# Low parts of split weights made by an accumulating DMA instead of a subtraction

## The chip, the cores and the metric

The kernel runs on one core of a Trainium2 chip. The metric is the device time of one execution in microseconds; the median of several runs is what counts, and a profile of one execution shows where the time goes. The engines are called PE (matrix product; PEld is its loading of weights), DVE (vector), ACT (scalar activation), POOL (GpSimd) and SP (issues DMAs).

## What is computed

Two transformer-like layers run over 128 context tokens and 512 latent tokens with the same weights. The layers differ in their mixer; both end in a gated feed-forward network (FFN) with a short convolution. All sizes are float32:

```python
for l in range(DEPTH):                      # DEPTH = 2, D_MODEL = 1024
    sh1, sc1, g1, sh2, sc2, g2 = split(silu(c) @ w_mod[l] + b_mod[l], 6)
    h = x * (1 + sc1) + sh1
    d = even_mixer(h) if l % 2 == 0 else odd_mixer(h)
    x = layernorm(ALPHA * x + g1 * d, ln1_g[l], ln1_b[l])
    h = x * (1 + sc2) + sh2
    z = dwconv(h @ w_up[l], conv_w[l], conv_b[l])      # 1024 -> 2 * 2816
    f = (silu(z[..., :D_FF]) * z[..., D_FF:]) @ w_down[l]
    x = layernorm(ALPHA * x + g2 * f, ln2_g[l], ln2_b[l])
```

The even mixer has an input projection, a spatial gate, pooling and an output projection; the odd mixer has a gated recurrence, attention with cached keys and an output projection.

## The kernel before

Every float32 product is made of three products of rounded numbers. An array x is split into a high part hi (x rounded to the type F32R) and a low part lo = x - hi. `mm3` (L150) then issues three matmuls for each pair of operands: hi times hi (L153), hi times lo (L154), lo times hi (L155). Activations are split where they are made. Weights come from HBM and are split as they are needed, each once, and this splitting is what the change touches.

A weight tile of 128 x 1024 (512 KB) passes through these steps. `want` (L112) puts its address on a queue; all weights of a stage are queued in the order of their use. `load` (L115) takes the next one and issues its DMA on SP into one of 4 buffers `r`. `prep` (L121) takes the oldest loaded tile and calls `split` (L96): ACT copies it with rounding into hi (L98), and POOL or DVE writes lo = r - hi (L101). Both parts lie in a pool of 12 buffers `w`, so six weights fit at a time. Which engine subtracts is chosen by the fourth argument of `want` or by the argument of `prep`; POOL is the default. `take` (L144) hands the oldest finished pair to the matmuls, and `pump` (L136) prepares ahead until `6 - hold[0]` pairs are ready. ACT, DVE and POOL each execute their instructions in order, so an instruction that waits holds up what stands behind it on its engine. A split runs under `high_priority`.

```python
    def prep(lo_eng=None):
        ...
        hi, lo = W(shape, F32R), W(shape, F32R)
        with tc.high_priority() if urgent[0] else ExitStack():
            i = split(hi, lo, raw, act, lo_eng or pool)
```

Only SP's order is written by hand (L44); the framework orders the instructions of the other engines by dependencies and priorities.

The stages follow each other: even mixer (0 to about 245 us in the profile), FFN of layer 0 (to about 750), odd mixer (to about 1110), FFN of layer 1 (to the end). In an FFN, PE alternates between up-projections, one weight and 48 matmuls at a time into two large PSUM buffers `A` (`ntile` L337; ACT and DVE make the convolution of one buffer in L527 to L529 and so free it), and down-projections of 3 or 4 weights held together (`down` L582, `project` L474). In a down-projection, or in an output projection (`out_proj` L613, two halves of four weights), every weight is used for all tokens, so buffers `w` become free only near its end. In the FFN of layer 0, DVE also works through the modulation of the next stages (L243). At the end of each stage stands a norm (`Norm`, L344): for each block of tokens DVE, POOL and ACT scale and shift it (L370 to L413), PE transposes it, and ACT and DVE split it (L430); the last block's rows are made by DVE in L392. A residual is scaled ahead on POOL in L449, and partial sums are added to it on POOL in L470.

Of the kernel before, what the change touches and what calls it, by code (L numbers as in the profile page):

```python
# [14 lines left out]
ALU = mybir.AluOpType  # L15
# [25 lines left out]
def tile_hybrid_trunk(ctx, tc, xT, x, vecs, tabs, wm0, wm1, wmT, crow, grow, lnrow, bs, w_u, w_v, w_p, w_s, w_pool, w_eo,  # L41
# [4 lines left out]
    dve, act, pe, pool, sp = nc.vector, nc.scalar, nc.tensor, nc.gpsimd, nc.sync  # L46
# [22 lines left out]
    def W(shape, dt=F32):  # L69
        return wpool.tile(shape, dt, tag="w", name=nm("w"))  # L70

    def R(shape):
        return rpool.tile(shape, F32, tag="r", name=nm("r"))
# [19 lines left out]
    def f(ap):  # L93
        return ap.bitcast(F32)

    def split(hi, lo, src, hi_eng, lo_eng):  # L96
        if hi_eng is act:
            act.copy(hi, src)  # L98
        else:
            hi_eng.tensor_copy(hi, src)  # L100
        return lo_eng.tensor_tensor(lo, src, f(hi), ALU.subtract)  # L101

# [1 line left out]
    queue = []  # L104
    ready = []
    loaded = []
    hold = [2]
    depth = [2]
    pin = [False]
    urgent = [True]  # L110

    def want(src, shape, scale=None, lo=None):  # L112
        queue.append((src, shape, scale, lo))

    def load():  # L115
        src, shape, scale, lo = queue.pop(0)
        raw = R(shape)
        sp.dma_start(raw, src)
        loaded.append((raw, shape, scale, lo))

    def prep(lo_eng=None):  # L121
        if not loaded:
            load()
        raw, shape, scale, lo_ = loaded.pop(0)
        lo_eng = lo_eng or lo_
        if scale is not None:
            dve.tensor_scalar(raw, raw, scale, ATTN_SCALE, ALU.mult, ALU.mult)
        hi, lo = W(shape, F32R), W(shape, F32R)
        with tc.high_priority() if urgent[0] else ExitStack():
            i = split(hi, lo, raw, act, lo_eng or pool)  # L130
        if pin[0]:
            tc.keep_in_program_order(i)
            pin[0] = False
        ready.append((hi, lo))
# [25 lines left out]
        pool.tensor_tensor(r, v, eps[:, 2:3], ALU.pow)  # L160
        return r

# [1 line left out]
    back = []  # L164

    def tick(n=1):
        for _ in range(n):
            while back:
                try:
                    next(back[0])  # L170
                    break
                except StopIteration:
                    back.pop(0)
# [2 lines left out]
        while len(back) > k:  # L176
            tick()

# [1 line left out]
    vec = cpool.tile([128, V_N], F32, name="vec")  # L180
    sp.dma_start(vec, vecs)
    ident = cpool.tile([128, 128], F32, name="ident")
# [9 lines left out]
    scr = [[dpool.tile([2, D], F32, name=f"scr{l}_{i}") for i in range(6)] for l in range(2)]  # L192
    SA1, SB1, SG1, SA2, SB2, SG2 = range(6)

# [1 line left out]
    def lnc(l, j):  # L196
        o = V_LN + (l * 4 + j) * 8
        return vec[:, o:o + 8].unsqueeze(1).to_broadcast([128, 2, 8])
# [5 lines left out]
    def rows_out(l, items):  # L204
        n = len(items)
        col = M([128, n, 2, 8])
        for q, (i, ap) in enumerate(items):
            dve.tensor_copy(col[:, q], ap)
        yield
        ps = B()  # L210
        pe.transpose(ps[:16 * n, :128], col.rearrange("p n s k -> p (n s k)"), ident)
        row = Tm([16 * n, 128])
        act.copy(row, ps[:16 * n, :128])
        for q, (i, ap) in enumerate(items):
            sp.dma_start(scr[l][i].rearrange("s (k f) -> (s k) f", f=128), row[16 * q:16 * q + 16, :])

    def finish_a(l):
        a, b, s = M([128, 2, 8]), M([128, 2, 8]), M([128, 2, 8])
        m = mc[l]
        dve.tensor_scalar(s, m[:, 1], 1.0, None, ALU.add)  # L220
        dve.tensor_tensor(a, s, lnc(l - 1, 2), ALU.mult)
        dve.tensor_tensor(b, s, lnc(l - 1, 3), ALU.mult)
        dve.tensor_tensor(b, b, m[:, 0], ALU.add)
        return rows_out(l, [(SA1, a), (SB1, b)])

    def finish_b(l):
        a, b, s = M([128, 2, 8]), M([128, 2, 8]), M([128, 2, 8])
        m = mc[l]
        dve.tensor_scalar(s, m[:, 4], 1.0, None, ALU.add)
        dve.tensor_tensor(a, s, lnc(l, 0), ALU.mult)  # L230
        dve.tensor_tensor(b, s, lnc(l, 1), ALU.mult)
        dve.tensor_tensor(b, b, m[:, 3], ALU.add)
        return rows_out(l, [(SA2, a), (SB2, b)])

    def mod_load(l, m, k, new):
        raw = new([128, D])
        sp.dma_start(raw, wmT[l, m * 8 + k])
        return raw

    def mod_cols(l, m, k, cb, raw):  # L240
        junk = Tm([128, D], mybir.dt.bfloat16)
        for s in range(2):
            op = dve.scalar_tensor_tensor(junk, raw, 1.0, cb[s], ALU.mult, ALU.mult, accum_out=mc[l][:, m, s, k:k + 1])  # L243
            if s == 0 and l == 1:
                tc.keep_in_program_order(op)

    def add_bm(l, m):
        dve.tensor_tensor(mc[l][:, m], mc[l][:, m], bmc(l, m), ALU.add)

    def mod_vec(l, ms, cb, new=R):  # L250
        todo = [(m, k) for m in ms for k in range(8)]
        raw = mod_load(l, *todo[0], new)
        yield
        for n, (m, k) in enumerate(todo):
            cur = raw
            if n + 1 < len(todo):
                raw = mod_load(l, *todo[n + 1], new)
            mod_cols(l, m, k, cb, cur)
            yield
            if k < 7:  # L260
                continue
            add_bm(l, m)
            if m == 1:
                yield from finish_a(l)
            elif m == 4:
                yield from finish_b(l)
            elif m == 2:
                yield from rows_out(l, [(SG1, mc[l][:, 2])])
            elif m == 5:
                yield from rows_out(l, [(SG2, mc[l][:, 5])])  # L270
            yield
# [44 lines left out]
    def ln_row(l, j):  # L316
        return bc_load(lnrow[:, (l * 4 + j) * D:(l * 4 + j + 1) * D])

# [1 line left out]
    def new_h():  # L320
        hi = [S([128, 2, T], F32R) for _ in range(4)]
        lo = [S([128, 2, T], F32R) for _ in range(4)]
        return hi, lo
# [14 lines left out]
        group(u, h, out, 0)  # L338
        group(u, h, out, 1)

# [1 line left out]
    ys = [None] * 5  # L342

    class Norm:  # L344
# [152 lines left out]
            norm.turn(4)  # L497
            pin[0] = True

# [1 line left out]
    def ffn(l, h):  # L501
        def plan():
            prev = None
# [124 lines left out]
                residual(norm)  # L628
        return nxt

# [1 line left out]
    def even_first(cb):  # L632
        want(w_v[0], [128, 2, 512])
        want(w_u[0], [128, D])
# [85 lines left out]
        for e in (dve, pool, dve):  # L720
            prep(e)
# [26 lines left out]
    def even_mixer(make_norm, nxt_sub):  # L748
# [28 lines left out]
        prep()  # L777
        load()
        prep(dve)
        back.append(mod_vec(0, (3,), cb, S))  # L780
        tick()
        for i in range(2, 5):
# [119 lines left out]
        nxt = out_proj(w_eo, ycat, gate, make_norm, nxt_sub, lambda i: pool_out(3, qs[3]) if i == 2 else None)  # L902
        return nxt, cb

# [1 line left out]
    def softplus_neg(lam):  # L906
        n = 8
        t, u, e, z, z2, s = (M([128, n]) for _ in range(6))
        dve.tensor_scalar(t, lam, -1.0, None, ALU.mult)
        dve.tensor_tensor(u, t, lam, ALU.max)  # L910
        act.activation(u, u, AF.Tanh, scale=1.0 / 32.0)
        dve.tensor_scalar(e, u, 1.0, None, ALU.add)
        dve.reciprocal(e, e)
        dve.tensor_scalar(u, u, -1.0, 1.0, ALU.mult, ALU.add)
        dve.tensor_tensor(e, e, u, ALU.mult)
        for _ in range(4):
            dve.tensor_tensor(e, e, e, ALU.mult)
        dve.tensor_scalar(z, e, 2.0, None, ALU.add)
        dve.reciprocal(z, z)
        dve.tensor_tensor(z, z, e, ALU.mult)  # L920
        dve.tensor_tensor(z2, z, z, ALU.mult)
        dve.tensor_scalar(s, z2, 1.0 / 17.0, 1.0 / 15.0, ALU.mult, ALU.add)
        for c in (13, 11, 9, 7, 5, 3, 1):
            dve.tensor_tensor(s, s, z2, ALU.mult)
            dve.tensor_scalar(s, s, 1.0 / c, None, ALU.add)
        dve.tensor_tensor(s, s, z, ALU.mult)
        dve.tensor_scalar(t, t, 0.0, None, ALU.max)
        dve.scalar_tensor_tensor(s, s, 2.0, t, ALU.mult, ALU.add)
        return s
# [10 lines left out]
    def odd_mixer(h):  # L940
# [98 lines left out]
        def rest(make_norm, nxt_sub):  # L1039
# [20 lines left out]
            raw = R([128, 2, 256])  # L1060
# [145 lines left out]
                qt.append(q)  # L1206
            uk = take()

            # attention: heads in pairs
            kts = [[[W([96, 896], F32R) for _ in range(2)] for _ in range(1 + hh)] for hh in range(2)]  # L1210
            for kt, e in zip(kts[0] + kts[1], ((dve, act), (dve, act), (dve, act))):
                for q in range(2):
# [96 lines left out]
            for n in range(len(steps) + 3):  # L1309
                if n < len(steps):  # L1310
                    j, hh, i = steps[n]
# [23 lines left out]
                if n >= 3:  # L1335
                    j, hh, i = steps[n - 3]
# [29 lines left out]
        eng.tensor_tensor(x1, a, b, ALU.subtract)  # L1366
        eng.tensor_tensor(x2, c, e, ALU.add)

# [1 line left out]
    def sub(maker, *args):  # L1370
        return lambda h: Sub(*maker(*args, h))

# [126 lines left out]
```

## Time and profile before

| | us |
|---|---|
| median of 3 runs | 1579.01 |
| the runs | 1576.65, 1579.01, 1590.5 |
| span of the profiled execution | 1581.2 |
| PE busy | 1473.5 |
| DVE busy | 1002.7 |
| POOL busy | 785.0 |
| ACT busy | 585.9 |

The span is that of one execution, from the first to the last instruction, and is the time against which sums are made here. Busy time is the union of an engine's instructions. A row of waits says for whom an engine sat idle. A row of a timeline gives start, duration, engine, line and operation, how many were merged (x), and in brackets how long the engine had been idle before it and what ended that.

### The profile page before, as it was taken

The numbers are of one execution on the slowest core, as the hardware profiler recorded it, in microseconds if no ns is written. First come the engines' busy times: TensorE is split into PE (matmuls) and PEld (weight loads), VectorE is DVE, ScalarE is ACT, GpSimd is POOL, SyncE is SP. The second block draws the span as 40 slices with busy tenths as digits, with TensorE's granted clock in tenths as the row PEclk, the third lists the DMA queues.
The fourth block names the chain that finished last, engine by engine and source line by source line (L and its number), as shares of the span: only waits on it lengthen the run. The fifth ranks groups of instructions, "written<-read, shape, count | busy, mean of one in ns | idle before, by whom it ended". The sixth has DMA issues, their size and how long they took to land. (4 is left out here: it accounts for less than half of the span.)

```text
span 1581.2 us, 21997 instructions
## 1 busy us (share of the span) xinstructions
PE 1473.5 (93%) x8741; PEld 1320.6 (84%) x8741; DVE 1002.7 (63%) x1432; ACT 585.9 (37%) x868; POOL 785.0 (50%) x564
## 2 busy tenths in 40 slices
PE   6889988899799999899979899998999999999997
PEld 3675868898799898887969788777999898999995
DVE  3485686577976778648688667858585342423347
ACT  3422354231323132324566465625334232322323
POOL 1132476634746466547367410576538816255444
PEclk9999999999999999999999899999999999999999
DMA  9345613243444353421220100352342421221311
GB/s 380 130 160 200 253 43 104 80 134 134 166 153 148 119 175 120 136 105 60 98 87 1 57 1 1 121 189 78 120 133 107 134 81 57 91 80 54 94 41 67
DMA packets 51734, 177.61 MB, mean 112 GB/s; under 512 B 6128, under 2 KB 6704, under 8 KB 51632
## 3 DMA queue, kind: packets, MB, share of 16 engines
q1 hardware_dynamic: 51632, 176.21, 32.6%
q8 instruction: 69, 1.13, 0.3%
q14 instruction: 33, 0.27, 0.1%
HBM read 170.71 MB, written 5.48 MB: 111 GB/s over the span
## 5 line engine op out<-in xcount | busy, mean ns | idle before, releaser
L101 POOL TENSOR_TENSOR w<-r,w 128x1024 fp32r<-128x1024 f32 (+2 forms) x148 | 369.8, 2508 | 465.6 <-ACT w L98 453.6
L153 PE MATMUL A<-s,w 128*128 128x258 f32 (+1 forms) x1672 | 525.9, 315 | 28.8 <-DVE t L529 19.2
L154 PE MATMUL A<-s,w 128*128 128x258 f32 (+1 forms) x1672 | 524.6, 314 | 3.8 <-DVE s L101 3.8
L155 PE MATMUL A<-s,w 128*128 128x258 f32 (+1 forms) x1672 | 523.9, 314 | 0.6 <-POOL w L101 0.6
L153 PEld LDWEIGHTS A<-s,w 128*128 128x128 f32 x1672 | 320.7, 192 | 41.0 <-issue 30.5
L98 ACT CAST w<-r 128x1024 fp32r<-128x1024 f32 (+3 forms) x184 | 186.6, 1029 | 389.1 <-PE B L154 168.3
L154 PEld LDWEIGHTS A<-s,w 128*128 128x128 f32 x1672 | 321.5, 192 | 7.7 <-DVE s L101 4.6
L155 PEld LDWEIGHTS A<-s,w 128*128 128x128 f32 x1672 | 320.8, 192 | 3.4 <-issue 2.5
L154 PE MATMUL B<-w,s 128*128 128x512 f32 (+2 forms) x734 | 283.2, 386 | 6.6 <-DVE w L101 6.6
L153 PE MATMUL B<-w,s 128*128 128x512 f32 (+2 forms) x734 | 283.5, 387 | 0.0
L155 PE MATMUL B<-w,s 128*128 128x512 f32 (+2 forms) x734 | 282.2, 384 | 0.0
L470 POOL TENSOR_TENSOR y<-y,t 128x512 f32<-128x512 f32 x120 | 183.0, 1537 | 112.9 <-DVE t L468 103.1
L528 DVE SCALAR_TENSOR_TENSOR t<-A,vec,t 128x641 f32<-128x641 f32 x88 | 77.7, 883 | 215.1 <-ACT t L527 210.2
L468 DVE TENSOR_TENSOR t<-B,s 128x512 f32<-128x512 f32 x160 | 108.7, 686 | 125.6 <-PE B L155 107.6
L243 DVE SCALAR_TENSOR_TENSOR t<-r,v 128x1024 bf16<-128x1024 f32 x112 | 185.2, 1658 | 2.9 <-DMA r<-in_wmT_dram 2.2
L154 PEld LDWEIGHTS B<-w,s 128*128 128x128 f32 x734 | 139.0, 189 | 34.4 <-DVE w L101 8.0
L155 PEld LDWEIGHTS B<-w,s 128*128 128x128 f32 x734 | 139.1, 190 | 27.4
L153 PEld LDWEIGHTS B<-w,s 128*128 128x128 f32 x734 | 139.1, 190 | 27.0 <-DVE t L468 0.2
L98 ACT CAST s<-t 128x642 fp32r<-128x642 f32 x60 | 43.8, 730 | 199.8 <-DVE t L538 166.9
L101 DVE TENSOR_TENSOR w<-r,w 128x1024 fp32r<-128x1024 f32 (+2 forms) x36 | 56.5, 1577 | 50.3 <-ACT w L98 50.2
L529 DVE SCALAR_TENSOR_TENSOR t<-A,vec,t 128x641 f32<-128x641 f32 x88 | 77.8, 885 | 2.7
L527 ACT ACTIVATE t<-A,vec 128x642 f32<-128x642 f32 x88 | 77.5, 881 | 5.0 <-PE A L155 4.5
(249 smaller groups left out, 1602.3 us busy)
## 6 DMA issues: line engine op xcount, KB each, us to landing
r<-in_w_up_dram SPq DMA_DIRECT2D x88, 512.0 KB, 3.6
r<-in_wmT_dram SPq DMA_DIRECT2D x56, 512.0 KB, 3.2
r<-in_w_dn_dram SPq DMA_DIRECT2D x44, 512.0 KB, 3.6
s<-scr SPq DMA_DIRECT2D x20, 512.0 KB, 6.6
s<-in_wm_dram SPq DMA_DIRECT2D x16, 512.0 KB, 9.3
r<-in_wm_dram SPq DMA_DIRECT2D x16, 512.0 KB, 4.4
s<-in_wmT_dram SPq DMA_DIRECT2D x8, 512.0 KB, 3.4
r<-in_w_eo_dram SPq DMA_DIRECT2D x8, 512.0 KB, 4.2
```

Of the source, the lines that this page charges most:

```text
L98: act.copy(hi, src)
L101: return lo_eng.tensor_tensor(lo, src, f(hi), ALU.subtract)
L153: pe.matmul(out, ah, bh, start=i == 0, stop=False)
L154: pe.matmul(out, ah, bl, start=False, stop=False)
L155: pe.matmul(out, al, bh, start=False, stop=i == n - 1)
L243: op = dve.scalar_tensor_tensor(junk, raw, 1.0, cb[s], ALU.mult, ALU.mult, accum_out=mc[l][:, m, s, k:k + 1])
L468: dve.tensor_tensor(t, ps, gate[stream(i)][:, sl], ALU.mult)
L470: pool.tensor_tensor(ys[i][:, sl], ys[i][:, sl], t, ALU.add)
L527: act.activation(t, z, AF.Identity, bias=cb, scale=w1)
L528: dve.scalar_tensor_tensor(t[:, 1:], z[:, :T - 1], w0, t[:, 1:], ALU.mult, ALU.add)
L529: dve.scalar_tensor_tensor(t[:, :T - 1], z[:, 1:], w2, t[:, :T - 1], ALU.mult, ALU.add)
```

## The change

From one point of the even mixer on (`through[0] = True`, after L779, when eight weights have been split), `prep` makes lo in another way, unless the weight is scaled first: ACT writes hi as before, ACT then writes lo = -hi, and a DMA issued by POOL adds the weight to lo, read from HBM a second time. The engine named in `want` no longer counts there; one named in `prep` still does. The remaining hunks of the diff delete comment lines.

```diff
+    through = [False]
@@ def load():
         sp.dma_start(raw, src)
-        loaded.append((raw, shape, scale, lo))
+        loaded.append((raw, shape, scale, lo, src))
@@ def prep(lo_eng=None):
-        raw, shape, scale, lo_ = loaded.pop(0)
-        lo_eng = lo_eng or lo_
+        raw, shape, scale, lo_, src = loaded.pop(0)
         if scale is not None:
             dve.tensor_scalar(raw, raw, scale, ATTN_SCALE, ALU.mult, ALU.mult)
         hi, lo = W(shape, F32R), W(shape, F32R)
         with tc.high_priority() if urgent[0] else ExitStack():
-            i = split(hi, lo, raw, act, lo_eng or pool)
+            if lo_eng or scale is not None or not through[0]:
+                i = split(hi, lo, raw, act, lo_eng or lo_ or pool)
+            else:
+                act.copy(hi, raw)
+                act.mul(lo, f(hi), -1.0)
+                i = pool.dma_start(lo, src, accum_op=ALU.add)
         if pin[0]:
             tc.keep_in_program_order(i)
             pin[0] = False
         ready.append((hi, lo))
@@ even_mixer
         prep(dve)
+        through[0] = True
         back.append(mod_vec(0, (3,), cb, S))
```

## Rows read from the trace of the kernel before

**Rows 1.** The page's first part: busy us (share of the span) xinstructions of each engine.

```profile
PE 1473.5 (93%) x8741; PEld 1320.6 (84%) x8741; DVE 1002.7 (63%) x1432; ACT 585.9 (37%) x868; POOL 785.0 (50%) x564
```

**Rows 2.** Who PE waited for: total us, times, longest us.

```profile
PE A L153 <- DVE t L529: 19.2, 9, 5.4
...
PE B L154 <- DVE w L101: 6.6, 4, 2.7
...
PE B L211 <- DVE m L208: 5.8, 5, 1.8
...
PE A L154 <- DVE s L101: 3.8, 1, 3.8
...
PE A L153 <- DVE t L826: 3.3, 1, 3.3
```

**Rows 3.** Windows: us, then PE, PEld, DVE, ACT, POOL busy, PEclk, DMA share, GB/s.

```profile
25.00:50.00 25.00, 20.95 (x140) 13.79 (x142) 10.42 (x23) 7.38 (x14) 4.70 (x2) 0.93 0.96 372
...
1175.00:1200.00 25.00, 25.00 (x171) 24.92 (x170) 18.19 (x21) 11.24 (x14) 9.79 (x4) 1.00 0.45 168
```

**Rows 4.** Groups by line and form: busy us, mean ns of one, idle before.

```profile
L101 POOL TENSOR_TENSOR w<-r,w 128x1024 fp32r<-128x1024 f32 x138 | 351.6, 2557 | 449.0 <-ACT w L98 437.1 <-DMA s<-in_wm_dram 11.8
...
L98 ACT CAST w<-r 128x1024 fp32r<-128x1024 f32 x170 | 175.6, 1047 | 382.0 <-PE B L154 168.3 <-PE A L154 124.8 <-DMA r<-in_w_up_dram 61.3
...
L101 DVE TENSOR_TENSOR w<-r,w 128x1024 fp32r<-128x1024 f32 x32 | 48.7, 1530 | 50.3 <-ACT w L98 50.2
...
L901 ACT ACTIVATE y<-y 128x1024 f32<-128x1024 f32 x5 | 5.2, 1056 | 1.9 <-DMA y<-in_x_dram 1.9
```

**Rows 5.** Timeline of POOL, DVE, ACT in the odd mixer's norm: start, us.

```profile
1105.21 10.28 POOL L101 TENSOR_TENSOR w<-r,w 128x1024 fp32r<-128x1024 f32 x4
...
1105.47 5.45 DVE L392 SCALAR_TENSOR_TENSOR t<-t,m,s 128x512 f32<-128x512 f32 x2
...
1104.55 1.05 ACT L98 CAST w<-r 128x1024 fp32r<-128x1024 f32 x1
```

**Rows 6.** Timeline of DVE in the last norm, where no weight is left.

```profile
1576.85 1.40 DVE L392 SCALAR_TENSOR_TENSOR t<-t,m,s 128x512 f32<-128x512 f32 x2
```

**Rows 7.** Timeline of DVE in the norms of the even mixer and of layer 0.

```profile
230.64 5.46 DVE L392 SCALAR_TENSOR_TENSOR t<-t,m,s 128x512 f32<-128x512 f32 x2
...
748.49 4.36 DVE L392 SCALAR_TENSOR_TENSOR t<-t,m,s 128x512 f32<-128x512 f32 x2
```

**Rows 8.** Timeline in the FFN of layer 0: DVE and the PE wait that follows.

```profile
404.60 2.56 DVE L243 SCALAR_TENSOR_TENSOR t<-r,v 128x1024 bf16<-128x1024 f32 x1
...
408.11 0.36 PE L153 MATMUL A<-s,w 128*128 128x258 f32 x1 [4.69 <-DVE t L529]
```

**Rows 9.** Timeline in the same stage: DVE beside POOL's scaling of the residual.

```profile
278.46 11.87 POOL L449 TENSOR_TENSOR y<-y,s 128x1024 f32<-128x1024 f32 x5
...
284.26 11.48 DVE L538 TENSOR_TENSOR t<-t,t 128x642 f32<-128x642 f32 x1
```

**Rows 10.** The core's span and mean granted clock.

```profile
core 0: 1581.2 us, clock 0.976
```

**Rows 11.** A window right behind that PE wait; columns as in rows 3.

```profile
408.60:412.00 3.40, 3.40 (x18) 3.40 (x18) 3.37 (x3) 2.33 (x3) 3.40 (x2) 0.51 0.10 39
```

**Rows 12.** Timeline of two places where weights come just in time.

```profile
1062.96 3.90 ACT L98 CAST w<-r 128x1024 fp32r<-128x1024 f32 x4 [21.04 <-PE B L154]
...
1064.05 2.81 DVE L101 TENSOR_TENSOR w<-r,w 128x1024 fp32r<-128x1024 f32 x2 [0.78 <-ACT w L98]
...
1542.43 1.60 DVE L101 TENSOR_TENSOR w<-r,w 128x1024 fp32r<-128x1024 f32 x1 [0.86 <-ACT w L98]
...
1066.70 0.39 PE L154 MATMUL B<-w,s 128*128 128x512 f32 x1
```

**Rows 13.** DMA issues: KB each, median us from issue to landing.

```profile
r<-in_w_up_dram SPq DMA_DIRECT2D x88, 512.0 KB, 3.6
...
s<-in_wm_dram SPq DMA_DIRECT2D x16, 512.0 KB, 9.3
```

## Prediction

> **What bounds the kernel now.** I read the page's busy times first. PE is busy for 1473.5 of 1581.2 us, so 107.7 us is all the idle time that any helper engine can give back; DVE, at 1002.7 us, is the busiest helper, POOL has 785.0 and ACT 585.9 [rows 1]. The cores' view adds that the mean granted clock is 0.976 [rows 10]. The clock has two levels, 1.2 and 2.4 GHz, so 2 x 0.024 x 1581.2 = 76 us ran at the lower one, and up to 38 us were lost by that. It falls behind idle stretches of PE: after the 4.69 us wait at 403 to 408 us [rows 8] the window shows 0.51 and 18 matmuls in 3.4 us [rows 11], where a full-speed window has 171 in 25 us, or 23 in 3.4 us [rows 3]. An idle microsecond of PE therefore often costs more than one.
>
> Then the waits of PE. The subtraction on POOL, the largest group outside PE with 138 x 2.557 us [rows 4], is hardly among them. What ends PE's idle time is DVE: 19.2 us for L529, 6.6 for low parts made on DVE, 5.8, 3.8 and 3.3 for smaller steps [rows 2]. The timelines show why DVE is late. In the odd mixer's norm L392 took 5.45 us for two instructions while POOL subtracted for 10.28 us [rows 5]; in the last norm, with no weights left, the same two took 1.40 us [rows 6]. In the FFN of layer 0, L243 took 2.56 us and L529, queued behind it, then released PE 4.69 us late [rows 8]. So a DVE instruction with two inputs in SBUF stands still while POOL reads SBUF. The Trainium skill's "SBUF — State Buffer" (Who interferes with whom) describes the shared port as an exclusive lock; the trace agrees, with 5.45 us against 1.40.
>
> **What the change removes.** From the code, 183 weights are queued, 8 are split before the switch and 3 are scaled, so 172 move: 140 from POOL and 32 from DVE. POOL loses about 140 x 2.56 = 358 us and DVE 32 x 1.53 = 49 us [rows 4], plus the time that it stands blocked. Five terms follow for PE.
>
> - Three norms: L392 falls to 1.40 us from 5.46, 4.36 [rows 7] and 5.45 [rows 5], together 15.27 - 4.20 = 11 us. PE waits at that point, so I take 11.
> - Behind the first of them PE waits 3.8 us for a low part on DVE [rows 2] that stands behind small blocked instructions: 4.
> - L529 in the FFN of layer 0: 19.2 us [rows 2], of which some 5 stem from L538 (11.48 us), blocked by POOL's L449 [rows 9], which stays. Of the other 14 I take 9, because POOL's L470 stays too.
> - The transposes of the modulation (5.8) and the gate's sum (3.3) [rows 2]: 6 of 9.
> - Clock: behind these gaps lie some 30 us at the lower level, as in [rows 11], at most 15 us lost. I take 10.
>
> Sum 40 us; if only half of the blocked time reaches PE it is 20, with all of it about 55 (11 + 4 + 14 + 9 + 15, rounded up).
>
> **What it adds on engines.** ACT writes 172 negated copies; the nearest row is a scaled 128 x 1024 ACT copy of 1.056 us (L901, [rows 4]), so 172 x 1.06 = 182 us at most, some tiles being smaller. In FFN stages this is covered: a weight is 48 matmuls, at 171 in 25 us 7.0 us [rows 3], in which ACT now works 11.24 / 25 x 7.0 = 3.1 us. Without that cover each copy would delay the convolution behind it by 1.06 us. In the norms ACT is on the path: three or four casts like the one at 1104.55 [rows 5] stand between ACT's critical steps, and half of the copies fall into its idle time. I take 2 us for each of three norms, 6 in all (0 to 12). POOL issues 172 DMAs. No DMA of POOL is in the trace; below lies nothing, above the subtraction that it replaces, 2.56 us, so POOL gains or stays even, and L470 behind an issue waits no longer than now, but for the 1.06 us that the copy makes POOL wait longer. I cost the issue's effect on the path at nothing, within a landing of 6 us below.
>
> **The late low parts.** This is the loss. The DMA reads 172 x 512 KB = 90 MB again; at 372 GB/s [rows 3] that is 1.4 us of all queues per tile, or twice that if lo is read as well. A plain load lands in 3.6 us, under full queues in 9.3 [rows 13]: these are the bounds for landing. I take 6: a load, plus 1.4 for the second read, plus 1 for the issue by POOL, being nearer to a load on half-empty queues. Low parts then come 1.06 + 6 = 7 us after the cast instead of 1.5 to 2.6. In FFN stages four pairs lie ready, 4 x 7.0 = 28 us ahead, and by the matching described below the shortest lead behind a down-projection is 11 us, so an extra 5 us is hidden there. It is not hidden where buffers `w` come free only at the end of a projection whose successor needs the next weight at once. At 1062.96 ACT casts, after 21 us of waiting for PE; the two DVE subtractions end at 1066.86; a matmul needing the first of them starts at 1066.70 [rows 12]. Matching every weight's subtraction to its first use, I count seven such places: the output projections of the even and the odd mixer (at 193, 1039 and 1067 us), the last down-projection of each layer (711 and 1545, the latter [rows 12]), one recurrence gate (807) and the attention's value weight (884). At each PE would be late by 7.06 - 1.6 = 5.5 us, and lose 1.7 us more while the clock is down (3.4 us at half, [rows 11]): 7 x 7.2 = 50 us. PE need not stand still, though: other token blocks and the weights at hand fill it for about 4 us, and the framework orders PE itself. I take half, 25 us; bounds are 10 (landing 3.6, mostly covered) and 72 (landing 9.3, nothing covered: 7 x (1.06 + 9.3 - 1.6 + 1.7) = 73).
>
> The Trainium skill prices this landing otherwise: "DMA: Bandwidth & Descriptors" (Anatomy of one DMA) has 2.0 us plus bytes over 436 GB/s for a DMA from GpSimd, an estimate of 3.2 us for 512 KB, and "Collectives: The Full Stack" (The bandwidth ceiling) halves the rate for an add, an estimate of 4.4 us. By 4.4 us the seven places cost 7 x 5.6 = 39, half of it 19, and the time would come to about 1564, inside the forecast's own range. No row here shows such a DMA.
>
> **The sum.** -40 + 6 + 25 = -9 us, against the span of 1581.2: 1572. The median of the runs lies 2.2 us below that execution (1579.0), so I say 1570. One per cent, 15.8 us, is about what a measurement of this kernel can tell from no change; the forecast is that the two cancel nearly.
>
> **Rivals.**
>
> 1. The late parts are hidden. PE's order, remade for the slower arrival, covers the seven places, and the loss falls to 10: -40 + 6 + 10 = -24, or with the full 55 us of gain -39, so 1540 to 1555. For it: DVE's blocking is plain in rows 5 to 9, and the seven places have work of other blocks at hand. Against it: PE B L154 waits 6.6 us for `w` even now [rows 2].
> 2. Landing decides against it. At the seven places four raw loads start as soon as the casts free their buffers, and the low parts share the queues with them. With no cover, the loss reaches 50 (no better than even with the gain of 40 - 6 = 34, slower by 1% from 34 + 16 = 50 on) at a landing of 6 us; with half of it covered, from about 13. At 9.3 us without cover: -40 + 6 + 73 = +39, 1618; with a third covered, about 1594 to 1600. For it: 9.3 us is measured in the opening, whose queues are 0.96 busy [rows 3, 13]. Against it: the rest runs at half that share or less.
> 3. The issue on POOL blocks DVE as the subtraction did, so the gain fails and the losses stay: 6 + 25 = +31, 1610. No row shows a POOL DMA; against it, it moves no tile through POOL.
> 4. The transfers bind. If one held all queues for longer than the 7.0 us of a weight, less 1.4 for its load, the FFN stages would slow with each weight: at 8 us, 132 weights x 2.4 = 317 us. I give that 3 in 100.
>
> **Chances and range.** Forecast (nearly cancelled, 1556 to 1590): 0.42. Rival 1: 0.30. Rival 2: 0.20. Rival 3: 0.05. Rival 4: 0.03. The likeliest case's own range is 1556 to 1590; the range for 8 in 10 takes in rival 1 and the near part of rival 2: 1538 to 1605. Faster by over 1% is a time below 1563: rival 1 and a small part of the forecast, 0.35. Slower by over 1% is above 1595: 0.26. Within: 0.39.
>
> **What the profile after would show.** POOL's L101 on `w` gone but for the first and the scaled weights, L392 at 1.4 us in all norms, L243 at about 1.2 us, PE's wait for L529 down to some 10 us. ACT near 765 us busy. New waits of PE at L154 and L155 for a DMA of `w`, at the seven places, 2 to 6 us each. If these waits are absent, rival 1 holds; if they exceed 6 us, rival 2; if L392 still takes over 4 us, rival 3; if PE in the FFN of layer 1 drops from its 25.00 us in 25 [rows 3], rival 4. The forecast is wrong above all if a landing takes less than 4 or more than 10 us, or if the remade order of the engines moves the norms by itself.

## The result

The changed kernel takes 1638.95 us (median; 1636.06 to 1644.11) against 1584.12 us for the kernel before on the same chip (four runs, among them the three whose median was 1579.01). The ratio is 1.037, with a 95% interval of 1.032 to 1.042: slower by 3.7%, where 1570 was forecast. Times of the experiments below are also compared by the ratio to the kernel before on their own chip; one point (0.01) is 15.8 us. Runs in the chip's slower state are left out of times and ratios; only e14 had one.

The page's first part of the kernel after, its mean clock, and its DMA queues (packets, MB, share of 16 engines' span), to be read beside [rows 1, 10]:

```profile
PE 1488.2 (91%) x8741; PEld 1334.6 (82%) x8741; DVE 879.4 (54%) x1400; ACT 751.5 (46%) x1040; POOL 571.9 (35%) x596
```

```profile
core 0: 1634.3 us, clock 0.956
```

```profile
q1 hardware_dynamic: 51632, 176.21, 30.8%
q0 software_dynamic: 24768, 88.75, 30.7%
```

Every helper did what the change asked: DVE lost 123 us of work, POOL 213, ACT gained 166. Yet PE's idle time rose from 107.7 to 1634.3 - 1488.2 = 146.1 us, and PE is busy 14.7 us longer for the same 8741 matmuls, while 2 x 0.044 x 1634 = 144 us of the span now run at the lower clock (76 before). These two, 38.4 + 14.7, are the whole 53.1 us between the spans. In the queues' rows, the new queue of POOL holds the 16 engines as long as all plain loads together, with half their bytes: 0.307 x 16 x 1634.3 / 24768 = 0.324 us for a packet.

Who PE waited for (total us, times, longest us), beside [rows 2]:

```profile
PE A L158 <- DVE t L534: 22.1, 6, 7.1
PE B L432 <- POOL t L418: 16.2, 5, 5.1
PE B L159 <- DMA w<-in_w_dn_dram: 15.0, 4, 10.7
PE B L159 <- DMA w<-in_w_oo_dram: 11.7, 3, 4.9
...
PE B L159 <- DMA w<-in_w_uv_dram: 6.8, 1, 6.8
PE A L160 <- DMA w<-in_w_rg_dram: 5.7, 1, 5.7
PE B L159 <- DMA w<-in_w_eo_dram: 5.3, 4, 3.1
...
PE B L159 <- DMA w<-in_w_qkv_dram: 4.3, 3, 2.5
```

All instructions of the new line L135 together: who waited for its DMAs (us, times), and the time from issue to landing:

```profile
PE B L159: 43.1, 15
...
PE A L160: 8.6, 2
...
DMA to landing us min/median/max: 4.0/7.5/15.6
```

Two costs stand out, then. PE waits 51.7 us, at 17 places, for a low part itself. And L534 still holds PE for 22.1 us (L529 held it for 19.2 before), though DVE no longer stands still beside subtractions of POOL, as its steps in the norms show; beside [rows 5, 7]:

```profile
240.10 0.78 DVE L397 SCALAR_TENSOR_TENSOR t<-t,m,s 128x512 f32<-128x512 f32 x1 [1.78 <-POOL m L165]
241.13 0.73 DVE L397 SCALAR_TENSOR_TENSOR t<-t,m,s 128x512 f32<-128x512 f32 x1
...
758.77 1.40 DVE L397 SCALAR_TENSOR_TENSOR t<-t,m,s 128x512 f32<-128x512 f32 x2
```

The other old cause is still there, and it makes the longest of the six waits. While POOL scales the residual (L454), DVE's L543 stands still as L538 did in [rows 9], L534 comes late behind it, and PE waits (timelines of DVE and PE):

```profile
271.51 10.37 DVE L543 TENSOR_TENSOR t<-t,t 128x642 f32<-128x642 f32 x1
...
289.26 0.55 PE L158 MATMUL A<-s,w 128*128 128x258 f32 x1 [7.15 <-DVE t L534]
```

What else holds L534 now is seen in a timeline of the FFN of layer 0 (start, us, engine, line; the engines one after the other), and behind it the time to landing of the one load in it:

```profile
427.61 1.04 ACT L133 CAST w<-r 128x1024 fp32r<-128x1024 f32 x1 [5.73 <-DMA r<-in_w_dn_dram]
428.56 0.88 ACT L532 ACTIVATE t<-A,vec 128x642 f32<-128x642 f32 x1
...
429.47 0.89 DVE L533 SCALAR_TENSOR_TENSOR t<-A,vec,t 128x641 f32<-128x641 f32 x1 [6.74 <-ACT t L532]
430.39 0.89 DVE L534 SCALAR_TENSOR_TENSOR t<-A,vec,t 128x641 f32<-128x641 f32 x1
...
414.43 0.33 SPq L119 DMA_DIRECT2D r<-in_w_dn_dram  x1
...
431.43 0.55 PE L158 MATMUL A<-s,w 128*128 128x258 f32 x1 [6.40 <-DVE t L534]
```

```profile
DMA to landing us min/median/max: 13.1/13.1/13.1
```

Read it backwards. PE starts at 431.43 after 6.40 us, because DVE's convolution (L533, L534) came late. DVE waited 6.74 us for ACT's L532. L532 itself waited for nothing: it stood in ACT's queue behind a cast of the next weight, and that cast waited 5.73 us for a plain load that had been issued at 414.43 and took 13.1 us to land. Four of the six waits, 14.3 us, have this form. So the new DMAs delay PE through the loads of other weights. The landing times of the large transfers (KB each, median us) say the same. Before, the raw loads of w_up took 3.6 us [rows 13], and those of w_dn:

```profile
r<-in_w_dn_dram SPq DMA_DIRECT2D x44, 512.0 KB, 3.6
```

After, with the new DMAs between them:

```profile
r<-in_w_up_dram SPq DMA_DIRECT2D x88, 512.0 KB, 5.4
w<-in_w_up_dram POOLq DMA_DIRECT2D x88, 512.0 KB, 7.9
...
r<-in_w_dn_dram SPq DMA_DIRECT2D x44, 512.0 KB, 7.8
```

The other new waits are plainer. In a norm (timeline of ACT, POOL and PE):

```profile
234.21 1.04 ACT L134 ACTIVATE w<-w 128x1024 fp32r<-128x1024 f32 x1
...
235.55 0.91 POOL L135 DMA_DIRECT2D w<-in_w_up_dram  x1 [4.69 <-ACT w L134]
236.18 1.57 POOL L415 TENSOR_TENSOR t<-y,s 128x512 f32<-128x512 f32 x1
237.83 1.73 POOL L418 TENSOR_TENSOR t<-t,s 128x512 f32<-128x512 f32 x1
...
239.61 1.12 PE L432 MATMUL B<-ident,t 128*128 128x128 f32 x4 [5.13 <-POOL t L418]
```

POOL stood 4.69 us at the issue of a DMA that needs ACT's negated copy, and the norm's own L415 and L418 stood behind it. And in the FFN of layer 1 the longest wait of all:

```profile
1253.88 7.45 POOL L454 TENSOR_TENSOR y<-y,s 128x1024 f32<-128x1024 f32 x3
1261.27 0.87 POOL L135 DMA_DIRECT2D w<-in_w_dn_dram  x1
...
1270.41 0.80 PE L159 MATMUL B<-w,s 128*128 128x512 f32 x1 [10.65 <-DMA w<-in_w_dn_dram]
```

The negated copy was done at 1259.52 (ACT's L134 began at 1258.48 and took 1.04). POOL, busy with scaling the residual, issued the DMA at 1261.27, and it landed about 9 us later.

### The profile page after: what moved, and what is told of

It reads as the page before. It is cut to its first block, busy times and chain, and to the rows that moved or that the text cites. A ratio compares the mean times of both kernels' runs of the same rounds, so it can differ in the third digit from the quotient of the medians.

```text
span 1634.3 us, 22380 instructions
## 1 busy us (share of the span) xinstructions
PE 1488.2 (91%) x8741; PEld 1334.6 (82%) x8741; DVE 879.4 (54%) x1400; ACT 751.5 (46%) x1040; POOL 571.9 (35%) x596
## 3 DMA queue, kind: packets, MB, share of 16 engines
q0 software_dynamic: 24768, 88.75, 30.7%
## 4 chain that ended last, share of the span: by engine, by line
PE 62%; DMA 12%; DVE 10%; POOL 7%; ACT 5%; issue 4%; SPq 0%; DVEq 0%; POOLq 0%; ACTq 0%
PE A L158 12%; PE A L160 12%; PE A L159 12%; PE B L159 7%; PE B L160 7%; PE B L158 7%; POOL y L454 2%; DVE t L248 2%; DMA r<-in_w_dn_dram 1%; DMA w<-in_w_dn_dram 1%; DMA r<-in_wm_dram 1%; DMA w<-in_w_eo_dram 1%; PE B L1280 1%; DMA r<-in_w_up_dram 1%; DMA t<-in_lnrow_dram 1%
## 5 line engine op out<-in xcount | busy, mean ns | idle before, releaser
L158 PE MATMUL A<-s,w 128*128 128x258 f32 (+1 forms) x1672 | 527.2, 316 | 26.4 <-DVE t L534 22.1
L133 ACT CAST w<-r 128x1024 fp32r<-128x1024 f32 (+2 forms) x172 | 177.4, 1032 | 383.8 <-PE B L159 179.6
L159 PE MATMUL B<-w,s 128*128 128x512 f32 (+2 forms) x734 | 290.0, 395 | 36.3 <-DMA w<-in_w_dn_dram 15.0
L158 PE MATMUL B<-w,s 128*128 128x512 f32 (+2 forms) x734 | 285.8, 392 | 5.5 <-ACT s L1108 3.8
L160 PE MATMUL B<-w,s 128*128 128x512 f32 (+2 forms) x734 | 286.4, 391 | 0.0
L533 DVE SCALAR_TENSOR_TENSOR t<-A,vec,t 128x641 f32<-128x641 f32 x88 | 77.9, 885 | 300.4 <-ACT t L532 300.4
L159 PEld LDWEIGHTS B<-w,s 128*128 128x128 f32 x734 | 142.2, 194 | 70.1 <-DMA w<-in_w_dn_dram 16.8
L134 ACT ACTIVATE w<-w 128x1024 fp32r<-128x1024 f32 (+2 forms) x172 | 178.7, 1039 | 1.7
L135 POOL DMA_DIRECT2D w<-in_w_up_dram x88 | 77.3, 908 | 288.5 <-ACT w L134 282.9
L158 PEld LDWEIGHTS B<-w,s 128*128 128x128 f32 x734 | 141.4, 193 | 34.6 <-ACT s L1108 4.1
L160 PEld LDWEIGHTS B<-w,s 128*128 128x128 f32 x734 | 142.4, 194 | 27.5
L248 DVE SCALAR_TENSOR_TENSOR t<-r,v 128x1024 bf16<-128x1024 f32 x112 | 154.8, 1386 | 0.7
L135 POOL DMA_DIRECT2D w<-in_w_dn_dram x44 | 38.0, 864 | 232.1 <-ACT w L134 221.6
L534 DVE SCALAR_TENSOR_TENSOR t<-A,vec,t 128x641 f32<-128x641 f32 x88 | 77.9, 885 | 2.7
```

Of the source, the lines that this page charges most:

```text
L133: act.copy(hi, raw)
L134: act.mul(lo, f(hi), -1.0)
L135: i = pool.dma_start(lo, src, accum_op=ALU.add)
L158: pe.matmul(out, ah, bh, start=i == 0, stop=False)
L159: pe.matmul(out, ah, bl, start=False, stop=False)
L160: pe.matmul(out, al, bh, start=False, stop=i == n - 1)
```

## The experiments

Three theories stood at the start: low parts come too late (1), ACT's second copy holds up norms and convolutions (2), and the traffic slows the raw loads (3). Two more came up on the way: the accumulation costs queue time (4), and each accumulating DMA has a fixed price (5). In each diff the lines replace those of the changed kernel, if nothing else is said.

**What the relief is worth, and what a DMA takes back.**

```diff
 e1_copy_only
-                act.mul(lo, f(hi), -1.0)
-                i = pool.dma_start(lo, src, accum_op=ALU.add)
+                i = act.mul(lo, f(hi), 2.0 ** -12)
 e2_early_plain_read
-                act.mul(lo, f(hi), -1.0)
-                i = pool.dma_start(lo, src, accum_op=ALU.add)
+                i = pool.dma_start(lo, src)
 e5_plain_read_waits
-                i = pool.dma_start(lo, src, accum_op=ALU.add)
+                i = pool.dma_start(lo, src)
```

> The changed kernel without its second read: ACT still writes a second tile per weight (a small multiple of the high part), but no DMA adds to it, so the low part is left out. Theory 1, the low parts come too late (PE's waits for a DMA of w sum to 51.6 us after the change): with them gone only the relief of DVE and POOL and the ACT copies stay, so about 1550 us (1584 - 40 + 6), and no PE wait for w over 2 us. Theory 2, ACT's second copy holds up the norms and the convolutions: the waits for L418 (16.2 us) and L534 (22.1 us) stay, and the time is 1575 to 1590.

> The second read stays, 512 KB per weight from POOL's queue, but as a plain read that waits for no cast and no ACT copy; the low part is then the whole weight, so the subtraction is left out. Theory 1 (late low parts): the read is early, so the loss goes and the time is 1545 to 1565. Theory 3, the traffic itself costs (raw loads w_up 3.6 to 5.4 us and w_dn 3.6 to 7.8 us to landing): ACT's casts and the convolutions behind them stay late, L534 stays near 22 us, and the time is 1595 or more.

> The changed kernel with a plain read in place of the accumulating one: the cast, the negated copy and the wait for it stay, but the DMA overwrites the low part with the whole weight, so the subtraction is left out. It splits the 75 us between the early plain read (1564) and the change (1639). Theory 1, the wait for the cast and the copy makes the parts late: 1615 to 1639. Theory 4, it is the accumulation (30.7% of the queues' time against 18.0% for the plain read of the same bytes): 1580 to 1600.

Measured: e1 1537.0 us, ratio 0.970 (0.966 to 0.975); e2 1563.6 us, 0.987 (0.986 to 0.989); e5 1575.9 us, 0.995 (0.992 to 0.997). The relief of DVE and POOL is real, 47 us with ACT's copies already paid, more than the 34 forecast; PE still waited up to 3.4 us for a part that ACT had just written, where theory 1 allowed 2. The early plain read was as theory 1 had it. The surprise is e5: a plain DMA of the same bytes, that waits for the same copy, still beats the kernel before. Theory 1 expected 1615 or more. So the wait for the copy does not by itself make the loss; 4.2 points, 67 us, lie between a plain and an accumulating DMA at the same place (63 by the medians). Some of this is lateness all the same, because the accumulating DMA lands later: 51.7 us of PE's waits for a low part are 32.3 in e5.

```profile
PE B L159: 27.4, 9
...
PE A L160: 4.9, 1
```

The layer-0 stage shows the difference best, cut from the first transposition of its norm to that of the next (windows: us, then PE, PEld, DVE, ACT, POOL busy, clock, DMA share, GB/s); in this order before, after, e1, e5:

```profile
208.00:726.00 518.00, 483.04 (x2817) 447.90 (x2815) 371.98 (x501) 157.84 (x201) 300.98 (x158) 0.98 0.37 123
```

```profile
215.00:736.00 521.00, 487.50 (x2817) 453.93 (x2815) 328.84 (x500) 222.48 (x268) 186.57 (x161) 0.96 0.73 189
```

```profile
196.00:676.00 480.00, 472.42 (x2813) 441.16 (x2812) 318.21 (x499) 222.84 (x267) 133.87 (x93) 1.00 0.40 133
```

```profile
203.00:689.00 486.00, 474.90 (x2821) 442.51 (x2820) 320.44 (x500) 222.75 (x267) 167.90 (x161) 0.99 0.61 202
```

This stage gives 38 us to e1 and loses 36 of them again between e5 and the change: the DMA engines go from 0.61 to 0.73 busy for the same bytes (486 us at 202 GB/s and 521 at 189 are both 98 MB). In e1 and e5 the wait for the convolution is almost gone:

```profile
PE A L157 <- DVE t L533: 0.8, 1, 0.8
```

```profile
PE A L158 <- DVE t L534: 4.3, 3, 3.2
```

All stages in us, cut in the same way, the last one up to PE's last matmul:

| | even mixer | layer 0 | odd mixer | layer 1 |
|---|---|---|---|---|
| before | 207.7 | 518.2 | 356.0 | 488.8 |
| after | 214.6 | 521.2 | 383.1 | 504.8 |
| e1, no DMA | 195.5 | 480.6 | 351.2 | 491.7 |
| e2, early plain read | 207.3 | 491.5 | 357.4 | 497.1 |
| e5, plain read | 203.4 | 485.4 | 373.4 | 497.9 |
| e13, read and write | 210.8 | 517.3 | 382.6 | 505.7 |
| e12, below | 194.6 | 501.1 | 356.2 | 488.8 |

In the odd mixer and in layer 1 it is otherwise: 17 of the 27 us and 9 of the 16 are lost with the plain read already. In the odd mixer that is the part of theory 1, for the same read without the wait takes 357.4 us (e2) or, with a copy that only the matmuls wait for (e6), 361.3. In layer 1 it is not: these take 497.1 and 496.1.

**ACT's second copy.**

```diff
 e3_copy_and_subtract
-                i = pool.dma_start(lo, src, accum_op=ALU.add)
+                i = (lo_ or pool).tensor_tensor(lo, raw, f(lo), ALU.add)
 e6_early_read_and_copy
-                act.mul(lo, f(hi), -1.0)
-                i = pool.dma_start(lo, src, accum_op=ALU.add)
+                act.mul(hi, f(hi), 1.0)
+                i = pool.dma_start(lo, src)
```

> The kernel before plus the ACT copy: the high part is negated by ACT as in the change, and POOL or DVE then adds the raw tile onto it, in place of the DMA. No second read. Theory 1 (late low parts): the copy delays a low part by about 1.05 us and is mostly hidden, 1584 to 1596. Theory 2 (ACT's copy in front of the norms and convolutions): 1600 to 1620.

> The early plain read with a second ACT pass over each weight that nothing but the matmuls waits for (the high part is rewritten in place); the low part is the whole weight, so the subtraction is left out. Theory 1 (lateness of the read decides): 1564 to 1575. Theory 2 (ACT's second pass delays norms and convolutions, once raw loads are slower too): 1590 or more.

Measured: e3 1601.7 us, 1.011 (1.008 to 1.014); e6 1568.6 us, 0.991 (0.989 to 0.994). Where POOL's work must wait for the second copy it costs 17.6 us in all, and PE's wait for L418 grows from 9.1 to 22.8 us (that for low parts from 8.5 to 12.1); where only the matmuls wait for it (e6 against e2), some 6. Most of the copy's price is therefore the waiting of POOL's queue, not ACT's time. Theory 2 is right in e3 and too dear in e6.

**Which weights, and how early.**

```diff
 e4_tight_on_dve
-            if lo_eng or scale is not None or not through[0]:
+            if lo_eng or lo_ or scale is not None or not through[0]:
 e7_negate_first
-                act.copy(hi, raw)
-                act.mul(lo, f(hi), -1.0)
-                i = pool.dma_start(lo, src, accum_op=ALU.add)
+                act.mul(lo, raw, -1.0)
+                i = pool.dma_start(lo, src, accum_op=ALU.add)
+                act.copy(hi, raw)
 e11_load_one_ahead
-    depth = [2]
+    depth = [3]
 e14_negate_from_raw
-                act.mul(lo, f(hi), -1.0)
+                act.mul(lo, raw, -1.0)
```

> The changed kernel, but the 32 weights whose low part DVE subtracted before are subtracted by DVE again; 140 keep the DMA. Theory 1 (late low parts): these are the weights used soon after their buffers come free (w_dn, w_eo, w_oo, w_qkv), so PE's waits for a DMA of w fall from 51.6 to about 20 us and the time to about 1600. Theory 3 (traffic): a fifth less traffic, 1625 or more.

> The change with ACT's two passes exchanged: minus the high part is made first, straight from the raw tile, then the high part. Every accumulating DMA can start one ACT pass (1.05 us) earlier. Theory 1 (lateness): seven or so places with 1.05 us less wait and a shorter spell at the lower clock, 1622 to 1632. Theory 3 or 4 (traffic or accumulation): 1635 to 1643.

> The changed kernel with three raw tiles loaded ahead instead of two, up to the middle of the odd mixer; the four raw buffers stay. If late raw loads hold ACT's in-order queue, and with it the convolutions of layer 0 (PE's wait for L534 22.1 us), one more load ahead gives 20 us or more back: 1600 to 1620. If the buffers or the queues are the limit rather than the moment of issue: 1632 to 1645.

> The change with its order of ACT's passes (high part first), but the negated copy reads the raw tile instead of the high part, so that a raw buffer comes free one ACT pass later. If negating first was slow (1683) because raw buffers came free later and the next raw loads with them: 1665 to 1690. If it was slow because the high part came later: 1635 to 1645.

Measured: e4 1603.2 us, 1.012 (1.010 to 1.014); e7 1683.2 us, 1.064 (1.058 to 1.069); e11 1646.3 us, 1.045 (1.041 to 1.050); e14 1663.1 us, 1.052 (1.046 to 1.058). With the 32 tight weights back on DVE, 40 of the 59 us return, and PE's waits for a DMA of a low part fall to 22.7, so these places matter, as theory 1 said, though with them goes a fifth of the accumulating. e7 was expected to gain and lost 42 us. Its L534 waits are 42.2 us, and ACT's waits for raw loads of w_up rise from 36.1 to 63.8 (they were 61.3 before the change, so such a wait costs only where PE needs what stands behind it). In e7 the raw tile is read by both of ACT's passes, so its buffer, one of four, comes free one pass later, and the next load with it. e14 changes that alone and loses 23 of those 42 us. Later raw loads thus cost time; the rest of e7's loss, perhaps a later high part, was not separated. e11 gave nothing back, though the loads came earlier to those that wait: ACT's waits for w_up and w_dn fell from 60.6 to 35.9 us and PE's for L534 from 22.1 to 17.3. In the layer-0 stage, 523.6 us long (521.2 in the change), PE's waits for low parts and for L216 grew by 6 us in their place. So the raw loads alone do not carry the loss.

**Queue time or a fixed price.**

```diff
 e9_half_tile
-                i = pool.dma_start(lo, src, accum_op=ALU.add)
+                h = shape[-1] // 2
+                i = pool.dma_start(lo[..., :h], src[..., :h], accum_op=ALU.add)
 e16_eighth_plain
-                i = pool.dma_start(lo, src, accum_op=ALU.add)
+                h = shape[-1] // 8
+                i = pool.dma_start(lo[..., :h], src[..., :h])
 e10_plain_read_twice
-                i = pool.dma_start(lo, src, accum_op=ALU.add)
+                i = pool.dma_start(lo, src)
+                pool.dma_start(dpool.tile(shape, F32, tag="x", bufs=4, name=nm("x")), src)
 e13_read_and_write
-                i = pool.dma_start(lo, src, accum_op=ALU.add)
+                i = pool.dma_start(lo, src)
+                pool.dma_start(dpool.tile(shape, F32, tag="x", bufs=8, name=nm("x")), f(hi))
```

e15_eighth_accumulated is e9 with `// 8`, and e17_half_plain is e16 with `// 2`.

> The changed kernel with the accumulating DMA over half of each tile's columns, 256 KB instead of 512; the other half keeps minus the high part, so half of the low parts is left out. Theory 4, the queue time of the accumulation slows the raw loads and makes the parts late: with half the bytes most of the 63 us between the plain read and the change go, 1575 to 1600, and DVE's L534 makes PE wait under 10 us. A fixed price of each accumulating DMA, or of its issue on POOL, instead: 1620 to 1640.

> The plain read that waits for the copy (1576) plus a second plain DMA of the same 512 KB from POOL's queue into DRAM that nobody reads; the low part is the whole weight, so the subtraction is left out. Queue time per weight is then about that of an accumulating DMA (18.3% becomes 30 to 37%), with no accumulation. Theory 4 as queue time: 1620 to 1645, raw loads of w_dn near 7.8 us. If accumulation costs by something else than its time on the queues: 1580 to 1600.

> The plain read that waits for the copy (1576) plus a second plain DMA of 512 KB from POOL's queue, here a write of the high part into DRAM that nobody reads, so that it cannot start before the cast as the doubled read did; the low part is the whole weight, so the subtraction is left out. POOL's queue then holds the queues about as long as the accumulating DMA does (288 us per queue for the plain read, 502 for the accumulating one, about 550 here). If queue time is what the accumulation costs: 1615 to 1645, raw loads of w_dn near 7.8 us, the stage of layer 0 near 520 us. If it costs by something else: 1578 to 1600, and that stage near 488.

> The changed kernel with the accumulating DMA over one eighth of each tile's columns, 64 KB; the rest keeps minus the high part, so seven eighths of the low parts are left out. Hardly any queue time is left, but all 172 accumulating DMAs and their issues on POOL (0.91 us each, 0.54 for a plain one). Theory 4, only bytes on the queues cost: 1550 to 1565, within 5 us of the plain eighth. Theory 5, a fixed price of each accumulating DMA of some 31 us in all (half a tile, with the queue time of a whole plain read, took 1.4% over the kernel before, the plain read 0.5% under it): 1575 to 1595, and 20 to 31 us above the plain eighth.

> The same with a plain DMA over the eighth (the copy, the wait and the 172 issues stay; nearly all of the subtraction is left out). It is the floor of a DMA that waits for the copy: 1550 to 1565 by both theories, between the kernel without a DMA (1537) and the plain read of whole tiles (1576).

> A plain DMA over half of each tile's columns, after the copy; the subtraction is left out. Its queue time is half of that of the half tile accumulated (which was 283 us per queue). Theory 4: some 16 to 20 us below the accumulated half (1.4% over the kernel before), so near 0.3% over it, 1588. Theory 5: 35 us or more below, 1568 to 1575.

Measured: e9 1598.8 us, 1.014 (1.012 to 1.017); e13 1623.8 us, 1.024 (1.019 to 1.029); e15 1581.1 us, 1.002 (1.000 to 1.004); e16 1563.5 us, 0.990 (0.987 to 0.994); e17 1569.9 us, 0.994 (0.991 to 0.996). e10 took 1854.9 us and decided nothing: its extra reads depend on nothing, the framework put them all into the opening, and PE's first real work waited 283.8 us; behind that, the three later stages took what they take in e5 (488.5, 372.0, 497.6).

| share of the tile | plain | accumulating | difference | PE's waits for low parts, us |
|---|---|---|---|---|
| none (e1) | 0.9705 | | | 5.1 |
| an eighth | 0.9902 | 1.0018 | 1.2 points, 18 us | 26.0, 32.4 |
| half | 0.9938 | 1.0144 | 2.1 points, 33 us | 29.0, 40.7 |
| all | 0.9948 | 1.0372 | 4.2 points, 67 us | 32.3, 51.7 |

The last column has the plain and then the accumulating kernel. A plain DMA costs 2.0 points for being there (waited for, issued by POOL, and landed before a matmul can use it), and its bytes next to nothing: from an eighth to all, 0.5 points. An accumulating one costs 18 us more at an eighth and 49 us more on top of that for the bytes.

Equal queue time splits the 67 us otherwise. The accumulating half of e9 holds each engine for 0.178 x 1588.1 = 283 us, the whole plain read of e5 for 288, and raw loads of w_dn land in 5.6 and 5.4 us; yet e9 is 2.0 points, 31 us, slower. So 36 to 49 us go with the bytes, as theory 4 has it, and 18 to 31 with any accumulating DMA, as theory 5 has it. The forecasts fit neither theory alone. Half a tile is in theory 4's range at 1598.8 us, and outside it by its ratio, 1607. e15 is 18 us above e16, where theory 4 said up to 5 and theory 5 said 20 to 31. e17 is 33 us below e9, where theory 4 said 16 to 20 and theory 5 said 35 or more.

The queue rows give the size of the queue time: a packet of the plain read holds an engine for 0.183 x 16 x 1572.3 / 24768 = 0.186 us, one of the accumulating read for 0.324. Here e5's queue, then e13's, which has no accumulation but twice the packets:

```profile
q0 software_dynamic: 24768, 88.75, 18.3%
```

```profile
q0 software_dynamic: 48896, 177.49, 30.1%
```

In e13 POOL's queue holds each engine for 0.301 x 1627 = 490 us, against 502 in the change and 288 in e5; raw loads of w_dn land in 7.1 us, the layer-0 stage takes 517 us, and 2.9 of the 4.2 points appear without any accumulation. Some of these belong to the second issue, and e13 also writes to HBM what the others do not: PE's wait for L419 is 27.0 us in e13, against 16.1 in e5.

For the fixed price two things are seen. POOL is busy longer with an accumulating issue, whatever its size (busy us, mean ns; e15, then e16):

```profile
L136 POOL DMA_DIRECT2D w<-in_w_up_dram x88 | 77.5, 909 | 280.3 <-ACT w L134 280.2
```

```profile
L136 POOL DMA_DIRECT2D w<-in_w_up_dram x88 | 47.7, 543 | 287.9 <-ACT w L134 287.7
```

And in the layer-0 stage, which holds 13.5 of the 18 us (495.0 against 481.5), one DVE instruction stands still while POOL scales the residual ten times in a row (L455), as one did before the change [rows 9]; e15, then e16:

```profile
260.19 15.92 DVE L544 TENSOR_TENSOR t<-t,t 128x642 f32<-128x642 f32 x1
```

```profile
272.05 2.69 DVE L544 TENSOR_TENSOR t<-t,t 128x642 f32<-128x642 f32 x1
```

The changed kernel and e9 have this too (10.37 us each), the plain e5 and e17 not (2.64 each); e13, plain with two issues, has 6.77. It costs PE 10.1 us in e15, and 7.15 in the change and in e9. Why DVE is caught in the one and not in the other, with POOL scaling in both, stays open, and so does the rest of the fixed price.

**Relief without a DMA.**

Both are the kernel before but for the engine that subtracts:

```diff
 e8_all_on_dve
-            i = split(hi, lo, raw, act, lo_eng or pool)
+            i = split(hi, lo, raw, act, lo_eng or dve)
 e12_dve_to_ffn0
+    count = [0]
-        lo_eng = lo_eng or lo_
+        lo_eng = lo_eng or lo_ or (dve if count[0] < 86 else None)
+        count[0] += 1
```

> The kernel before with every low part subtracted by DVE, none by POOL: no second read, no ACT copy. If the gain of 47 us without low parts came from DVE's blocking by POOL's subtractions (95 us of DVE's excess time), DVE does 140 x 1.1 to 1.5 us more but is blocked less: 1555 to 1575. If DVE's queue decides, the added 150 to 210 us come before norms and convolutions: 1590 to 1620.

> The kernel before with DVE making the low parts of the first 86 weights (even mixer and feed-forward of layer 0), and POOL and DVE sharing the rest as before. From the stages, even mixer 194 and layer-0 stage 502 us as with all on DVE, odd mixer 356 and layer-1 stage 489 as before, with 11 us ahead of the first matmul: about 1553. If the gain was the lock on DVE, it stands here without the price that DVE paid in the odd mixer; if all on DVE won for another reason, 1566 or more.

Measured: e8 1566.2 us, 0.990 (0.987 to 0.993); e12 1553.9 us, 0.986 (0.983 to 0.988), which beats both kernels. DVE makes the low parts of 104 tiles of 1024 columns in e12,

```profile
L101 DVE TENSOR_TENSOR w<-r,w 128x1024 fp32r<-128x1024 f32 x104 | 145.5, 1405 | 115.2 <-ACT w L98 109.9 <-PE B L290 5.0
```

where it made 32 [rows 4], and is busy only 1022.5 us in all, 20 more than before, although these subtractions take 97 us more: its other work takes some 77 us less. The odd mixer stays as it was in e12 (356.2 us), while in e8 it took 364.4; there DVE has no room.

## Why the prediction was wrong

The step that failed is the price of the DMA. It was put at 25 us, all of it for seven late low parts; between e1, which has everything but the DMA, and the change lie 1.0372 - 0.9705 = 6.7 points, 106 us. The gain was there, and larger than forecast.

- **The gain, 40 us less 6.** Its mechanism was right and it was too small. L397 fell to 1.40 to 1.51 us in all norms as forecast, the transposes' wait nearly went (L213 0.4 us) and the gate's went, and e1 measures 47 us net. L248 fell to 1.386 us, not 1.2. For L529 I took 9 of 19.2 us and left some 5 to POOL's scaling of the residual; in e1 0.8 us of the wait is left, and in the change the scaling alone makes 7.15.
- **ACT's copies, 6 us.** Mis-sized. I counted ACT's time in the norms; the cost is mostly POOL's in-order queue waiting for the copy. e3 puts the whole at 17.6 us.
- **"I cost the issue's effect on the path at nothing."** Wrong. A plain DMA of an eighth, which lands in 2.9 us at the median, costs 2.0 points, 31 us, over e1: PE waits 17.6 us for POOL in the norms instead of 5.6, and 26.0 us for low parts instead of 5.1. An accumulating issue takes POOL 0.91 us. The wait at 1259.76 (10.65 us, and 7.65 with the plain read of e5) and most of those for L418 come from here.
- **The late low parts, 25 us.** Mis-sized, and the largest term. The landing was taken as 6 us; its median is 7.5, its longest 15.6. Seven places were counted; PE waited at 17, for 51.7 us. Some 34 us of it lie at the weights of the seven places, where 7 x 5.5 = 39 was the full price without the clock, so other work covered far less than the half that was taken. The other 18 us lie where nothing was expected. (The upper bound is written as 72; its sum gives 73.)
- **The step that was missing.** The DMA was priced by its own landing alone. That it delays other transfers stood only in rival 4, and there only if one DMA held all queues for a whole weight. Far less suffices: w_dn's raw loads went from 3.6 to 7.8 us, and ACT's queue passed that on to the convolution, 14.3 us of PE's waits. "An extra 5 us is hidden there" held nearly for the low parts of the layer-0 stage (4.9 us of waits) and not for the raw loads beside them. That stage, the source of 38 us of gain, ended 3 us longer than before. How the 67 us that the accumulation adds divide between queue time and a fixed price is known only as the range above, and what makes the fixed price is open.
- **The clock, 10 us gained.** It went the other way: 144 us of the span at the lower level instead of 76, so up to 34 us more lost.
- **The rivals.** Rival 1 (hidden) falls. Rival 2 had the sign and shared queues, and its highest price, 73 us, was still below the 106. Rival 3 falls as told: a DMA of POOL does not block DVE as the subtraction did (L397). Rival 4 falls as told: PE is busy 25.00 of 25 us in most of layer 1's FFN, with single long waits between.
- **The Trainium skill's price.** The Trainium skill's pages "DMA: Bandwidth & Descriptors" (Anatomy of one DMA) and "Collectives: The Full Stack" (The bandwidth ceiling) gave an estimate of 4.4 us for the landing, 3.2 without the add. Here the medians were 7.5 and, for the plain read of e5, 5.0, with the queues shared. The two differ by 2.5 us; in packet time the add costs a factor of 1.74. The second of these pages of the Trainium skill halves the rate of a reduction, because its add reads two sources; 1.74 is near that.

## What to carry to other kernels

Moving work to a DMA moves it into a queue that other transfers use: price what the new traffic does to the transfers that are there, and follow these into the in-order engines that wait for them. Measure the gain and the price apart, as e1 does here. A DMA issued by a busy compute engine is issued when that engine's queue gets to it, and everything behind it waits for what the DMA waits for. If a lock between two engines is what hurts, first try to give all of that work to one of the two in the stages where it has room; here that was worth 1.4% and needed no new transfer.

## What was not expected of the hardware

An accumulating DMA from HBM into SBUF held the DMA engines 1.74 times as long per packet as a plain one (0.324 against 0.186 us), landed in 7.5 instead of 5.0 us at the median, and its issue took POOL 0.91 instead of 0.54 us at any size from 64 to 512 KB. POOL's ten scalings in a row held one DVE instruction for up to 15.92 us, in some orders of the same work and not in others.
